# Hybrid encoder trunk on one core: even projections of two groups by seven products, two scan streams, division at the gates

## The chip, the core and the metric

The kernel runs on one core of a Trainium2 chip. The metric is device time of one execution in microseconds. All matrix work is float32 split into a rounded high part and a low part (`F32R`), so that one float32 product is three TensorE matmuls: high x high, high x low, low x high.

The engines are named as in the profile: PE is TensorE (PEld its weight loads), DVE is VectorE, ACT is ScalarE, POOL is GpSimd, SP is SyncE, whose queue issues every DMA.

## The reference

Two requests (2048 and 512 tokens, 1024 features) go through the same two layers. The first is the even one, the second the odd one:

```python
def even_sublayer(x, w_in, ...):
    u = x @ w_in
    qa, ka, va, za, gd, qb, kb, vb, zb = jnp.split(u, _offsets(EVEN_SPLITS), axis=-1)
    ya = gla_mixer(qa, ka, va, za, gd, ...)      # gated linear attention, chunks, both directions
    yb = swa_mixer(qb, kb, vb, zb, rel_bias, sink)   # softmax over |i-j| <= 128
    return jnp.concatenate([ya, yb], axis=-1) @ w_out

def swa_mixer(...):
    ...
    e = jnp.exp(s - m)
    p = e / (jnp.sum(e, -1, keepdims=True) + jnp.exp(sk - m))
    o = jnp.einsum('bnkgqs,bnskd->bnqkgd', p, vb)
    return o * jax.nn.silu(z)

def odd_sublayer(x, w_in, conv_w, w_out):
    bg, cg, h, z = jnp.split(x @ w_in, 4, axis=-1)
    conv = ...                                   # width-3 convolution of cg * h
    return (jax.nn.silu(z) * bg * conv) @ w_out

x = layer_norm(DN_ALPHA * x + sublayer(x))       # after each layer
```

## The kernel before

The 2560 tokens are five groups of 512 (0 to 3 the long request, 4 the short one) and 20 chunks of 128.

**Stages.** PE works through a list of dense stages (`run`, L2103). For each group of the even layer there are `tok` (`e1_tok`: values and decay inputs, 336-column matmuls) and `ch` (`e1_ch`: 21 channel units, each 24 matmuls of 512 columns against the group's transposed activations). `oe` and `oo` are the output projections of the even and the odd layer with residual and norm, `one` is the odd layer's input projection of group 4, and `pair` that of two groups at once. The order before is tok 4, ch 4, tok 3, ch 3, tok 2, ch 2, tok 1, ch 1, oe 4, tok 0, ch 0, one, oe 0, oo 4, oe 1, oe 2, pair 0, oe 3, oo 0, pair 1, oo 1, oo 2, oo 3.

**Pairs by seven products.** `odd_pair` computes a 2x2 block product (two halves of the inner dimension by two groups, two weight units) with seven half-size products instead of eight, in the order 1, 6, 7, 5, 2, 4, 3. Each product is 12 matmuls. `pair_weights` makes the sums of weight quarters and their high and low parts (ACT casts, POOL subtracts), `prep_pair` those of the activations.

**Side work.** Between dense matmuls the planner (`Flow`, L263) steps generators. `gla_stream` runs the scan: for each chunk, last to first, `inside` multiplies queries and keys by decays level by level (spans 1, 2, 4, 8, 16, 32, 64) on DVE, with small 32x32 and 64x64 matmuls for each level, then the chunk's output and state; `along` goes forward once all chunks of a request are through. `swa_front` computes scores and exponentials of a block (a chunk and one of two key heads; 40 in all) and divides by the row sum; `swa_back` transposes, multiplies by the values and then by the gates `gb` and stores to `mix_s`. `prep` loads transposed activations into three `pr` buffers and splits them into `st` tiles, of which there are eight: two groups' worth.

**What sets the order.** The planner has its own clocks for the engines; a generator is stepped when the data it named should be ready. The resulting order is fixed at build time on each engine. SP issues DMAs in that order, and one that waits holds all behind it. Stage gates are marks such as `gla_in3` (all inputs of group 3's scan stored), `swa_3` (chunk 3's attention stored), `bias` (the relative-bias tables loaded).

**Lines.** L242 is the helper through which every instruction of an engine is recorded, so all rows of the profile have this line; they are told apart by tile names: `acc` and `ps` are PSUM banks, `ws`/`y` raw weights, `wh`/`wl` their high and low parts, `md`/`pr` work buffers, `st` split activations, `QQ`/`KK` the scan's queries and keys, `P` attention probabilities, `den` their row sums.

## Time and profile before

| what | value |
|---|---|
| median of 3 runs | 2370.76 us (2369.61 to 2370.84) |
| profiled execution, its own time | 2370.12 us |
| span of that execution | 2368.1 us |
| PE busy | 2343.9 us (99%), 15830 records |
| DVE busy | 1582.8 us (67%) |
| ACT busy | 1226.1 us (52%) |
| POOL busy | 1418.4 us (60%) |
| granted TensorE clock | 0.998 of full speed |
| DMA | 437.37 MB, mean 185 GB/s |

The span runs from the first to the last instruction; the execution's own time has some 2 us around it. Busy shares are means over the whole run; a window table gives them by stage. A group's row has its count, its busy time and mean ns of one, then the idle time of the engine before these instructions and who ended it. A timeline row has start and length in us. DMA rows have the median time from issue to landing.

### The profile page before, as it was taken

Reading aid. Unit: us, or ns where it says so; the run is one execution under the profiler, and the core shown is the slowest. Engines: PE = TensorE matmul, PEld = TensorE weight load, DVE = VectorE, ACT = ScalarE, POOL = GpSimd, SP = SyncE. Lnnn points to the kernel's source line nnn. Section 1 sums busy time; section 2 is a strip of 40 time slices with the busy share of each in tenths; the row PEclk is TensorE's granted clock in tenths of the full one; section 3 lists DMA queues with packets and bytes.
Section 4 is the critical chain, followed back from the end, with each engine's and each line's share of the span. In section 5 each row is a group of like instructions: output and inputs, shape, how many; then the busy total and the mean of one; then the engine's idle time right before and its main releaser. Section 6 shows DMA issues by size and latency. Waiting matters only on the chain.

```text
span 2368.1 us, 43087 instructions
## 1 busy us (share of the span) xinstructions
PE 2343.9 (99%) x15830; PEld 1951.8 (82%) x15830; DVE 1582.8 (67%) x2699; ACT 1226.1 (52%) x2363; POOL 1418.4 (60%) x1610
## 2 busy tenths in 40 slices
PE   8999999999999999999999999999999999999998
PEld 8888889888988888888888888878888877888887
DVE  2267756767767677577776467876566587656567
ACT  4666776656576645665577532543334343333431
POOL 5454435443444444444444467898887689988674
PEclk9999999999999999999999999999999999999999
DMA  7977686676667657675478777232124633221573
GB/s 230 295 226 233 221 269 229 209 221 221 218 194 236 223 173 242 197 218 161 158 245 268 266 261 243 92 116 89 52 78 140 217 105 103 73 72 58 175 242 121
DMA packets 275057, 437.37 MB, mean 185 GB/s; under 512 B 21360, under 2 KB 160240, under 8 KB 274848
## 3 DMA queue, kind: packets, MB, share of 16 engines
q1 hardware_dynamic: 274848, 434.64, 56.5%
q8 instruction: 125, 2.05, 0.4%
q14 instruction: 84, 0.69, 0.1%
HBM read 319.72 MB, written 114.84 MB: 184 GB/s over the span
## 4 chain that ended last, share of the span: by engine, by line
PE 87%; DVE 5%; POOL 4%; DMA 2%; issue 1%; ACT 1%; SPq 0%; POOLq 0%; DVEq 0%; ACTq 0%
PE acc L242 71%; PE ps L242 17%; POOL wl L242 1%; POOL wh L242 1%; DVE st L242 1%; DVE bst L242 1%; DVE y L242 1%; POOL md L242 0%; SPq L242 0%; DVE QQ L242 0%; DVE P L242 0%; DVE KK L242 0%; DMA K<-kb_s 0%; DMA mix_s<-gb 0%; DMA op_s<-QQ 0%
## 5 line engine op out<-in xcount | busy, mean ns | idle before, releaser
L242 POOL TENSOR_TENSOR wl<-ws,wh 128x256 fp32r<-128x256 f32 (+1 forms) x912 | 750.7, 855 | 711.4 <-PE acc L242 478.0
L242 PE MATMUL acc<-st,wh 128*128 128x512 f32 x3160 | 828.5, 395 | 2.8 <-DVE pr L242 2.0
L242 PEld LDWEIGHTS acc<-st,wh 128*128 128x128 f32 x3160 | 580.9, 188 | 121.0 <-issue 3.1
L242 PE MATMUL acc<-st,wl 128*128 128x512 f32 x1744 | 471.9, 395 | 2.8 <-POOL wl L242 1.9
L242 PE MATMUL acc<-wh,st 128*128 128x512 f32 (+1 forms) x1680 | 389.4, 371 | 7.9 <-ACT st L242 6.4
L242 PEld LDWEIGHTS acc<-st,wl 128*128 128x128 f32 x1744 | 320.8, 188 | 68.0 <-POOL wl L242 4.1
L242 PEld LDWEIGHTS acc<-wh,st 128*128 128x128 f32 x1680 | 300.2, 189 | 55.1 <-ACT st L242 6.4
L242 ACT CAST wh<-ws 128x1024 fp32r<-128x1024 f32 (+2 forms) x252 | 249.0, 989 | 184.2 <-DMA ws<-in_w_oo 55.9
L242 PE MATMUL acc<-wl,st 128*128 128x512 f32 (+1 forms) x840 | 209.0, 368 | 0.6 <-POOL wl L242 0.5
L242 ACT ACTIVATE md<-md 128x512 f32<-128x512 f32 x264 | 164.7, 631 | 20.5 <-DVE md L242 14.9
L242 PEld LDWEIGHTS acc<-wl,st 128*128 128x128 f32 x840 | 150.7, 188 | 23.8 <-POOL wl L242 1.3
L242 DVE SCALAR_TENSOR_TENSOR md<-acc,md 128x512 f32<-128x512 f32 (+1 forms) x113 | 77.0, 683 | 81.5 <-ACT md L242 76.5
L242 DVE TENSOR_TENSOR st<-pr,st 128x512 fp32r<-128x512 f32 x115 | 98.5, 874 | 41.6 <-ACT st L242 41.2
L242 ACT ACTIVATE md<-acc 128x512 f32<-128x512 f32 (+1 forms) x133 | 76.2, 597 | 67.0 <-PE acc L242 66.5
L242 POOL TENSOR_TENSOR wh<-md,wh 128x256 fp32r<-128x256 f32 x118 | 96.7, 842 | 13.6 <-ACT wh L242 13.1
L242 ACT CAST pth<-ps 128x512 fp32r<-128x512 f32 x112 | 65.3, 583 | 73.1 <-PE ps L242 72.3
L242 DVE CUSTOM_DVE_ANT_0 P<-ps,P 128x384 f32<-128x384 f32 (+1 forms) x160 | 79.3, 525 | 29.6 <-PE ps L242 29.0
L242 ACT ACTIVATE P<-P,nm 128x385 f32<-128x385 f32 (+1 forms) x160 | 93.2, 587 | 3.9 <-DVE nm L242 3.9
L242 ACT ACTIVATE mv<-mv,eps 128x1 f32<-128x1 f32 x40 | 11.8, 295 | 151.8 <-DVE mv L242 147.7
L242 PE MATMUL acc<-P,wh 128*128 128x512 f32 x312 | 89.5, 400 | 0.4 <-POOL wh L242 0.4
L242 ACT COPY km<-KK 128x512 f32<-128x512 f32 x80 | 50.8, 635 | 72.2 <-DVE KK L242 50.9
L242 ACT CAST st<-pr 128x512 fp32r<-128x512 f32 x115 | 68.3, 617 | 30.3 <-DMA pr<-mix_s 12.9
(490 smaller groups left out, 4090.2 us busy)
## 6 DMA issues: line engine op xcount, KB each, us to landing
ws<-in_w_ch SPq DMA_DIRECT2D x105, 512.0 KB, 4.4
ws<-in_w_od SPq DMA_DIRECT2D x58, 512.0 KB, 4.2
ws<-in_w_oe SPq DMA_DIRECT2D x40, 512.0 KB, 3.8
ws<-in_w_oo SPq DMA_DIRECT2D x36, 512.0 KB, 3.5
K<-kb_s SPq DMA_DIRECT2D x32, 384.0 KB, 6.3
d_s<-md SPq DMA_DIRECT2D x40, 256.0 KB, 4.2
qb_s<-md SPq DMA_DIRECT2D x80, 128.0 KB, 3.9
tA<-d_s SPq DMA_DIRECT2D x20, 512.0 KB, 5.7
```

The source lines that it names most:

```text
L242: r = f(*a, **k)
```

## The change

**Seven products in the even layer.** Groups 4 and 3 now run together: tok 4, tok 3, then unit 0 of both groups plainly, then 20 units as ten pairs by seven products (`even_pair`), then tok 2 and the rest as before. `prep_even` loads the transposed activations of both groups once more, makes four sums per 128-row slab on DVE and their high and low parts. The parts are kept in the buffers of local attention (`P`, `Q`, `pth`, `ptl`, `gb`, `K0`, `K1`, `V`) until the last pair. `pair_weights` is made general for both uses and keeps fewer sums.

**The scan as two streams.** `inside` ends after the levels; a second generator `gla_behind` does the chunk's output and state. A chunk's levels can run while the chunk before is finished. Keys and queries may use `y` buffers, copies may use `md` buffers. Level 2's queries are copied aside, and the blocks of levels 2 and 4 are multiplied together into one PSUM bank, as those of 8 and 16 were already.

**Division at the gates.** The probabilities are no longer divided. The reciprocal row sums go to DRAM (`rd_s`), are read back as rows broadcast over 64 partitions, and POOL multiplies the gates by them.

Local attention's set-up also moves: its bias tables are loaded when products 6, 7 and 5 of the last pair are done. Other edits: the loop over late work is rewritten, a plain product holds its PSUM bank, `dtot` has eight columns.

The core of the diff:

```diff
+    def prep_even(self, a, b):
...
+        places = early + self.half
+        todo, raws, last = [(k, i, g) for k in range(4) for i in range(2) for g in (a, b)], [], []
...
+        for k in range(4):
...
+            b11, b12, b21, b22 = raws
+            t = self.take(places, (128, 512))
+            sub(t[:], b12[:], b11[:])
+            sub(b12[:], b22[:], b12[:])
+            sub(b22[:], b22[:], t[:])
+            sub(b21[:], b21[:], b22[:])
...
+            for n, r in ((6, b22), (7, b12), (5, t)):
+                hi[n].append(cell())
+                lo[n].append(cell())
+                split(n, k, r, None)
+                yield []
+        yield "plain_e"
+        hi[4], lo[4] = self.big_cells(), self.big_cells()
...
+    def even_pair(self, groups, units, take, put, decay):
...
+        for n, cts in enumerate(units):
+            u = {"ct": cts}
+            for i in (1, 6, 7, 5, 2, 4, 3):
+                if n == 0 and i in (4, 5, 6, 7):
+                    yield "paire_%d" % i
...
+                for k in range(4):
+                    c = slice(k * 128, k * 128 + 128)
+                    nc.tensor.matmul(p[:], w[:, 0, c], H[i][k], start=(k == 0), stop=False)
+                    nc.tensor.matmul(p[:], w[:, 0, c], L[i][k], start=False, stop=False)
+                    yield
+                for k in range(4):
+                    c = slice(k * 128, k * 128 + 128)
+                    nc.tensor.matmul(p[:], w[:, 1, c], H[i][k], start=False, stop=(k == 3))
...
     def setup_bias(self):
...
+        for i in (6, 7, 5):
+            yield "free_paire_%d" % i
...
     def inside(self, c, first, last, ld, K, ahead):
...
-            if s in (8,):
+            if s in (2, 8,):
...
+        self.heads.append((c, first, last, K, Q, base, acmp))
+        self.flow.mark("head_%d" % c)
...
     def swa_front(self):
...
-                for h in range(4):
-                    nc.vector.tensor_scalar(Pt[:, h, :w], Pt[:, h, :w], den[:, h:h + 1], None, op0=ALU.mult)
-                    if h == 1:
-                        yield []
+                nc.sync.dma_start(self.rd_s[c, kv].rearrange("h t -> t h"), den[:])
...
     def swa_back(self):
...
+            for j in range(4):
+                nc.sync.dma_start(rb[64 * kv:64 * kv + 64, 128 * j:128 * j + 128],
+                                  self.rd_s[c, kv, j:j + 1].broadcast_to([64, 128]))
...
+            yield [gb, rb]
+            flat = gb[:].rearrange("p h t -> p (h t)")
+            nc.gpsimd.tensor_tensor(flat, flat, rb[:], op=ALU.mult)
...
     def run(self):
...
-        stages = [("tok", 4), ("ch", ((4,), A + B)), ("tok", 3), ("ch", ((3,), A + B)),
+        even = [(1, 2), (3, 4), (5, 6), (7, 8), (13, 14), (15, 16), (9, 10), (11, 12), (17, 18), (19, 20)]
+        stages = [("tok", 4), ("tok", 3), ("ch", ((4, 3), [0], even)),
                   ("tok", 2), ("ch", ((2,), A + B)), ("tok", 1), ("ch", ((1,), A + B)), ("oe", 4),
```

**How the order moves, first place: PE and SP at the first channel units.** PE before, from the end of the first token projection (`gd` are the decay inputs, `y` the decay weights):

```order
L242 MATMUL acc<-wl,st 128x336 x2
L242 MATMUL acc<-st,wh 128x512 x16
L242 MATMUL acc<-st,wl 128x512 x8
L242 MATMUL acc<-ident,gd 32x128 x4
L242 MATMUL acc<-st,wh 128x512 x16
```

PE in the changed kernel, from the end of group 3's token projection; `relb` is the relative bias, and `P`, `Q`, `gb` hold the sums of slabs 0 and 1, 2, and 3:

```order
L242 MATMUL acc<-wl,st 128x336 x2
L242 MATMUL acc<-st,wh 128x512 x16
L242 MATMUL acc<-st,wl 128x512 x8
...
L242 MATMUL acc<-st,wh 128x512 x8
L242 MATMUL ps<-QQ,relb 8x512
L242 MATMUL acc<-st,wh 128x512 x4
L242 MATMUL acc<-P,wh 128x512 x4
L242 MATMUL acc<-Q,wh 128x512 x2
L242 MATMUL acc<-gb,wh 128x512 x2
```

The plain units are followed at once by products of sums, and the relb matmul stands inside product 1. SP in the changed kernel at that place (`S`, `A` and `pr` receive the last slab; `KK` is the bias line):

```order
L242 DMA relb<-in_relb 32x8
L242 DMA pr<-in_xT 128x512
L242 DMA S<-in_xT 128x512
L242 DMA A<-in_xT 128x512
L242 DMA k_s<-md 128x4x128
L242 DMA line_s<-KK 8x512
L242 DMA pr<-in_xT 128x512
```

In the order before, the line's store stands among the stores of the first token projection and no activations are loaded here. The fourth load of the last slab now stands behind it.

**Second place: SP at oe 0.** Before, where the last result of `one` (`od_s`) is stored (`tA`, `QQ` and the like are the forward scan's loads):

```order
L242 DMA ws<-in_w_oe 128x1024
L242 DMA pr<-od_s 128x512 x3
L242 DMA P<-in_x 128x1024
L242 DMA od_s<-md 128x512
L242 DMA mix_s<-KK 512x1x128
```

In the changed kernel:

```order
L242 DMA pr<-mix_s 128x512 x3
L242 DMA ws<-in_w_oe 128x1024
L242 DMA mix_s<-qn 512x1x128
...
L242 DMA rd_s<-den 128x4x1
L242 DMA od_s<-md 128x512
L242 DMA QQ<-op_s 128x512
L242 DMA QQ<-qf_s 128x512
L242 DMA qn<-ga_s 128x512
L242 DMA pr<-mix_s 128x512
L242 DMA pr<-od_s 128x512
```

Before, all eight loads of `mix_s` for oe 0 stand ahead of this piece and the `pr` buffers already serve the next stage; now three stand just ahead of it and five behind the last `od_s` store, among loads of `od_s`.

More of the change, by code (lines that the diff above doesn't have):

```diff
@@ L296, in flush @@
     def flush(self, everything=False, name=None):
-        now, keep = [], []
-        for one in self.late:
-            (now if everything or name in one[2] or (name is None and one[0] <= self.t) else keep).append(one)
-        self.late = self.model.late = keep
+        now = [one for one in self.late if everything or name in one[2] or (name is None and one[0] <= self.t)]
         for one in now:
-            one[1]()
+            if any(one is x for x in self.late):
+                self.late[:] = [x for x in self.late if x is not one]
+                one[1]()
     def force(self, *tiles):
@@ L804, in prep @@
         raws = []
-        eager, homes = homes is not None, homes or self.half
+        eager, homes = homes is not None, homes or self.half + (self.mids if wide else [])
         todo = list(range(8))
@@ L1034, in e1_tok @@
         gd = self.gd[g] = self.sm((128, 4, 32), "gd")
-        stores = {"gla_in": 24, "swa_in": 29, "done_sw": 33, "done_e1_": 37}
+        names = ["gla_in", "swa_in", "done_sw", "done_e1_"] if g < 3 else ["gla_in", "done_e1_", "swa_in", "done_sw"]
+        stores = {n: 24 + sum({"swa_in": 5}.get(x, 4) for x in names[1:i + 1]) for i, n in enumerate(names)}
         def left(what):
@@ L1075, in e1_ch @@
         if us[0] == 0:
-            if groups == (4,):
+            if 4 in groups:
                 yield "up"
@@ L1150, in take @@
                           lambda: put(g, dst, h, o, "done_e1_" if u < 17 else "done_sw"))
-            if 1 < u < 10:
-                decay(g, (u - 2) // 4, (u - 2) % 4)
+            for i in () if units else {7: (6, 7)}.get(u, (u - 1,) if 0 < u < 7 else ()):
+                decay(g, i // 4, i % 4)
         for u in us:
@@ L1161, in e1_ch @@
                 yield
-            if u == 9:
+            if u == 7 and not units:
                 self.drop(up, *(G[g] for g in groups))
@@ L1165, in e1_ch @@
                 G.clear()
+        if units:
+            own = self.owned["e1_%d" % groups[1]]
+            self.drop(*own[:2])
+            del own[:2]
+            flow.mark("plain_e")
+            yield from self.even_pair(groups, units, take, put, decay)
         if u == 16:
@@ L1178, in gla_load, with gla_home @@
         return q, T1
+    def gla_home(self, tag):
+        done = self.flow.done
+        rows = "late_e1_1" in done and "res_x1_4_3" not in done
+        return [(self.e2, tag, 1)] if rows or self.model.spare(tag, 1) else self.large[:1]
     def gla_load_k(self, c):
-        K = self.e((128, 2, 512), "KK")
+        K = self.take(self.gla_home("KK"), (128, 2, 512))
         for i in range(2):
@@ L1232, in inside @@
         base = None
-        Sb = self.bst if not last else None
         wait = []
@@ L1314, in inside, with load_v, behind @@
                     nc.vector.copy_predicated(acmp[:], self.lmask[:, lt].unsqueeze(1).broadcast_to([128, 4, 32]), x)
-            if s == 4:
-                v = self.e((128, 512), "v")
-                nc.sync.dma_start(v[:], self.v_s[c])
+            if s in (4, 32):
+                ahead(s)
             yield [Q] if s < 16 else [Q, K]
-        end = tots[128]
+        nc.vector.tensor_copy(self.dtot[:, c], mk(tots[128], 0, [[1, 8]]))
+        self.heads.append((c, first, last, K, Q, base, acmp))
+        self.flow.mark("head_%d" % c)
+    def load_v(self, c):
+        v = self.e((128, 512), "v")
+        self.nc.sync.dma_start(v[:], self.v_s[c])
+        return v
+    def behind(self, c, first, last, K, Q, base, acmp, v, ahead):
+        nc = self.nc
+        Sb = self.bst if not last else None
         A = self.e((128, 4, 128), "A")
@@ L1349, in inside @@
                                   acmp[:].unsqueeze(2).broadcast_to(wide))
+        self.open -= 1
         if not first:
-            yield from self.bank()
+            yield from place()
             kb = turn(1)
-        ahead(1)
+        self.drop(K)
         yield [A, v] + ([Sb] if Sb is not None else [])
@@ L1452, in seq, with gla_behind, ahead @@
         return (0, 16) if g < 4 else (16, 20)
+    def gla_behind(self):
+        nxt = []
+        for c in [*range(19, 15, -1), *range(15, -1, -1)]:
+            yield "head_%d" % c
+            v = nxt.pop() if nxt else self.load_v(c)
+            def ahead():
+                if c not in (0, 16) and "gla_in%d" % ((c - 1) // 4) in self.flow.done:
+                    nxt.append(self.load_v(c - 1))
+            yield from self.behind(*self.heads.pop(0), v, ahead)
+            v = None
     def gla_stream(self):
+        nxt = {}
@@ L1900, in total @@
             def total(name, x, y, op):
-                while self.free_at(self.mids) > flow.t:
-                    yield 0.3
-                t = sums[name] = self.take(self.mids, (128, 512))
                 c = self.model.clock
                 e = nc.gpsimd if c["gpsimd"] + 0.6 < c["vector"] else nc.vector
+                if name in (3, 7):
+                    e.tensor_tensor(y, x, y, op=op)
+                    sums[name] = y
+                    yield [m[1] if name == 7 else held[0]]
+                    return
+                places = self.mids if p != "e" or n == 0 else self.half + (self.early if n < 4 else self.large)
+                while self.free_at(places) > flow.t:
+                    yield 0.3
+                t = self.take(places, (128, 512))
+                held.append(t)
+                sums[name] = t[:]
                 e.tensor_tensor(t[:], x, y, op=op)
@@ L1912, in pair_weights @@
                     yield from total(5, quarter(1, 0), quarter(1, 1), ALU.add)
-                    yield from total(6, sums[5][:], quarter(0, 0), ALU.subtract)
+                    yield from total(6, sums[5], quarter(0, 0), ALU.subtract)
                 elif i == 7:
```

298 lines of the change are left out of this document (240 added, 58 removed).

## Prediction

> **What bounds the kernel now.** I read the profile in this order: the page's busy times, the table by stages, the chain of waits, the groups by form, the waits of each engine, then the timeline at two stage entries. The span and the busy times come first.
>
> ```profile
> span 2368.1 us, 43087 instructions
> PE 2343.9 (99%) x15830; PEld 1951.8 (82%) x15830; DVE 1582.8 (67%) x2699; ACT 1226.1 (52%) x2363; POOL 1418.4 (60%) x1610
> ```
>
> TensorE (PE) is busy for 2343.9 of 2368.1 us. The 24.2 us left are not a reserve in the middle: the first matmul starts at 6.44 us and the last ends at 2360.3, which leaves some 10 us for all waits between.
>
> ```profile
> 6.44 0.65 PE L242 MATMUL acc<-wh,st 128*128 128x336 f32 x1 [6.44 <-ACT st L242]
> 2359.90 0.40 PE L242 MATMUL acc<-P,st 128*128 128x512 f32 x1
> ```
>
> The table by stages (window; then busy us of PE, PEld, DVE, ACT, POOL; clock; DMA share; GB/s) says the same of every stage. The four windows are the first channel projections, the next 200 us, the main part of the attention, and the first stage of the odd layer that already uses seven products.
>
> ```profile
> 60.00:160.00 100.00, 100.00 (x672) 81.58 (x671) 41.37 (x71) 63.27 (x99) 52.43 (x69) 1.00 0.88 275
> 160.00:360.00 200.00, 200.00 (x1746) 171.58 (x1745) 135.13 (x314) 139.42 (x314) 86.74 (x112) 1.00 0.73 232
> 760.00:1300.00 540.00, 538.89 (x4352) 450.83 (x4351) 387.46 (x790) 328.59 (x724) 240.47 (x294) 1.00 0.65 209
> 1551.00:1886.00 335.00, 334.73 (x1460) 274.76 (x1461) 210.30 (x255) 129.41 (x187) 278.12 (x288) 0.99 0.32 108
> ```
>
> PE fills each of them; DVE never has over 72% of a window (387 of 540), and POOL is near its limit only in the last (278 of 335). So a microsecond of matmul that goes is a microsecond won, as long as no new wait stands in its place, and relief of DVE alone is worth nearly nothing. What one 512-column matmul costs is read from the chain of waits (start, length, what), in that last window:
>
> ```profile
> 1551.27 334.56 PE acc L242 x1456
> ```
>
> 334.56 / 1456 = 0.230 us each. (The 395 ns of the groups overlap, since matmuls are pipelined.)
>
> **What the change removes.** Twenty of the 21 channel units of groups 4 and 3 were 2 x 20 x 24 = 960 matmuls of 512 columns; ten pairs of units at seven products of 12 matmuls are 840. The other TensorE work (token projections, scan blocks, scores, transposes) keeps its counts and shapes. 120 x 0.230 = 27.6 us go. The profiled execution took 2370.12 us (its span and 2.0 around it; the median of the runs is 2370.76, 0.6 above), so the bare sum is 2342.5 us. Everything else has to be hidden or added. Edits that move no time go together: the new loop over late work, held PSUM banks in the plain products, eight columns of decay totals, decays one unit earlier, the order of the marks.
>
> **The first 85 us: 0.** Group 3's activations now have to be there when group 4's token projections end, and 16 more slabs of 256 KB are loaded for the sums.
>
> ```profile
> 0.00:60.00 60.00, 53.40 (x284) 48.10 (x285) 16.54 (x33) 25.56 (x42) 34.18 (x56) 1.00 0.72 229
> ```
>
> By the changed SP queue, loads and stores up to the entry add up to about 22 MB in 85 us, 260 GB/s. The rows of before show 229 in the first 60 us and 275 in the next 100 with PE full; so it fits, and what it costs if it doesn't is the landing time in the next part.
>
> **Entry of the seven products: +7.5 us.** The product order is 1, 6, 7, 5, 2, 4, 3. Product 1 uses plain activations; product 6 needs the sums of all four column slabs of xT. In the changed SP queue the last slab's last load stands behind the store of the relative-bias line, and that store waits for a DVE add, which waits for the small relb matmul; PE has that matmul in the middle of product 1. The rows that price this chain:
>
> ```profile
> 37.72 0.68 DVE L242 TENSOR_TENSOR pth<-ps,gb 8x512 f32<-8x512 f32 x1 [0.87 <-PE ps L242]
> 40.24 0.39 SPq L242 DMA_DIRECT2D line_s<-pth  x1
> pr<-in_xT SPq DMA_DIRECT2D x35, 256.0 KB, 4.7
> md<-in_xT SPq DMA_DIRECT2D x5, 256.0 KB, 6.5
> L242 DVE TENSOR_TENSOR st<-pr,st 128x512 fp32r<-128x512 f32 x115 | 98.5, 874 | 41.6 <-ACT st L242 41.2
> ```
>
> From the end of the relb matmul: 0.68 (the add, 37.72), 0.39 (the store's issue, 40.24), 4.7 from the load's issue to its landing, then in DVE's order two subtractions that make the sum, one that is queued between, and the low half, 4 x 0.87 = 3.5. That is 9.3, with some 0.5 for five hand-offs 9.8. PE still has four matmuls of product 1 and six of product 6 to do, 2.3 us; 7.5 us of wait remain. No row shows this wait, as the stage isn't there. A wait of PE can't be below 0; at most the landing takes 6.5, as in the slowest group of xT loads, and DVE comes 3 us late: 12. I take the sum of the medians.
>
> **Entry of the first output projection after the odd layer's group 4: +6 us.** Local attention now starts when the products release the P buffers, near 300 us instead of at 126 (its bias tables were loaded there), and still has 40 blocks to do; before, its last store was at 1261. The projection's loads of mix_s now stand behind the 18th of attention's 20 stores. Before (timelines of SP and PE):
>
> ```profile
> 126.15 0.98 SPq L242 DMA_DIRECT2D P<-bias_s  x2
> 1261.09 0.53 SPq L242 DMA_DIRECT2D mix_s<-gb  x1
> 1263.46 1.60 SPq L242 DMA_DIRECT2D pr<-mix_s  x3
> 1287.44 1.37 SPq L242 DMA_DIRECT2D pr<-mix_s  x1
> 1310.95 0.33 SPq L242 DMA_DIRECT2D ws<-in_w_oe  x1
> 1321.02 0.32 SPq L242 DMA_DIRECT2D od_s<-md  x1
> 1319.65 3.90 PE L242 MATMUL acc<-wh,st 128*128 128x512 f32 x16
> 1326.12 3.79 PE L242 MATMUL acc<-wh,st 128*128 128x512 f32 x16
> pr<-mix_s SPq DMA_DIRECT2D x40, 256.0 KB, 4.8
> L242 ACT CAST st<-pr 128x512 fp32r<-128x512 f32 x115 | 68.3, 617 | 30.3 <-DMA pr<-mix_s 12.9 <-DMA pr<-od_s 7.0 <-DMA pr<-in_xT 6.5
> ```
>
> The eight loads went out from 1263 to 1288, 32 to 56 us ahead of the stage at 1319.65. Now three stand just ahead of the stage's second weight load (at 1310.95, 8.7 us ahead): landing, cast and low half take 4.8 + 0.62 + 0.87, 6.3 in all, so these come in time. The fourth stands behind the last od_s store (1321.02, 1.4 after the start) and three more loads of about 0.4: issued at 2.7, ready at 9.0. The stage wants it when its second weight block begins, 6.5 after the start (1326.12). That is 2.5 us. The other four stand further back, between weight loads, and share three pr buffers with the next stage's od_s loads; I give the two later pairs 1.7 each. Sum some 6. From below, 0, if the loads find their buffers early; from above, if each of three pairs is a whole landing late, 14.
>
> **Weights in the new stage: 0, hidden.** POOL now makes 140 low halves and 22 sums there. Rows for the halves and the sums:
>
> ```profile
> L242 POOL TENSOR_TENSOR wl<-ws,wl 128x256 fp32r<-128x256 f32 x44 | 48.1, 1113 | 12.3 <-ACT wl L242 12.0
> L242 POOL TENSOR_TENSOR wh<-y,wh 128x256 fp32r<-128x256 f32 x32 | 37.5, 1194 | 2.0 <-ACT wh L242 1.8
> L242 POOL TENSOR_TENSOR wl<-QQ,wl 128x256 fp32r<-128x256 f32 x10 | 13.6, 1377 | 4.3 <-ACT wl L242 4.3
> L242 POOL TENSOR_TENSOR wh<-md,wh 128x256 fp32r<-128x256 f32 x118 | 96.7, 842 | 13.6 <-ACT wh L242 13.1
> L242 POOL TENSOR_TENSOR md<-ws,md 128x512 f32<-128x512 f32 x9 | 11.7, 1297 | 0.0
> ```
>
> By the names in the changed order half of them read from y at about 1.2 us, the rest at 0.84 to 1.11: 140 x 1.09 + 22 x 1.30 = 181 us, against 840 x 0.230 = 193 of products and some 10 of side matmuls. 22 us of PE hide what POOL lacks in evenness. If each half took the longest row, 1.38, POOL would need 222 and the stage would be 19 us longer; that is a rival. The Trainium skill, in "SBUF — State Buffer", section "Who interferes with whom", says that a DVE instruction with two SBUF inputs and a GpSimd instruction that reads SBUF exclude each other for their whole length. The trace agrees in kind (the same 128x256 form takes 842 ns in one group and 1377 in another), and by that rule the scans, which now run beside this stage, would bring that rival's time.
>
> **Local attention: 0.** Per block four DVE divisions go:
>
> ```profile
> L242 DVE TENSOR_SCALAR P<-P,den 128x384 f32<-128x384 f32 x128 | 61.6, 543 | 1.1
> L242 DVE TENSOR_SCALAR P<-P,den 128x256 f32<-128x256 f32 x32 | 10.9, 405 | 0.3
> L242 POOL TENSOR_TENSOR gb<-gb 128x512 f32<-128x512 f32 x20 | 27.3, 1367 | 61.4 <-DVE gb L242 61.4
> ```
>
> 72.5 us of DVE go, and 20 POOL multiplications of 1.37, 27 us, come. Both lie beside PE; the relief can win at most the 10 us of waits that PE has, and if POOL's cover in the attention were gone (240 of 540 us busy), the 27 would show. I take neither. SP gets 40 stores of reciprocals and 160 short loads. At about 0.4 us each that is 80 us of issue in 1000, and a read waits on SP until its store has landed; weight loads queue behind. What they have in reserve:
>
> ```profile
> SPq L242 <- POOL wl L242: 490.1, 195, 7.4
> SPq L242 <- DVE den L242: 9.1, 3, 4.5
> ACT wh L242 <- DMA ws<-in_w_ch: 43.0, 19, 7.2
> ```
>
> SP mostly waits for a weight buffer to come free (490 us), so loads go out as early as they can; and ACT has waited 43 us for such weights without PE feeling it. From below nothing is won; from above half a microsecond per block, 20 us. I take 0, as the nearest row (SP waiting 9.1 us in all for den) is small. The Trainium skill, in "DMA: Bandwidth & Descriptors", section "Rules for kernel authors", says that a strided last dimension is lowered to one descriptor per element; the reciprocals are stored that way, 512 elements of four bytes. No run here shows such a store.
>
> **The scans: 0.** They start in the middle of the new stage instead of at about 110 us, as two streams; levels 2 and 4 make one PSUM bank instead of two. Their matmul count stays and no long stretch of the new order has scan work without projection matmuls between. Their cover is DVE's 28% in the attention; if that were gone, the wait would show at the entry priced above.
>
> Sum: 2370.1 - 27.6 + 7.5 + 6 = 2356.0 us.
>
> **The rivals.** One: no new wait. Loads land sooner and DVE runs ahead; PE stays as full as in the windows above. 2370.1 - 27.6 = 2342.5, say 2343. For it: in the trace of before entries cost next to nothing. Against it: the order of the SP queue, which no speed of DVE changes. Two: POOL sets the pace of the new stage. If the halves take 1.25 on average, POOL needs 140 x 1.25 + 29 = 204, no cover is left and unevenness shows: 10 to 19 us, so 2366 to 2375, about the time of before. For it: the y and QQ rows; against it: 278 of 335 us in the like stage, where PE lost nothing. Three, on the other side: SP held by reciprocals. Where a read stands close behind its own store, SP waits up to a landing, 4 us, and weight loads come late. From 0.5 us of PE per block on (2375.5 - 2356 = 19.5 over 40) the kernel is slower than before; at 0.75 it takes 2386. For it: the changed order puts reads as near as three rows behind their store; against it: SP's reserve above.
>
> **How the numbers follow.** A measurement of this kernel can tell about 0.2%, 4.7 us: faster is below 2366.0, slower above 2375.5. Chances: forecast 0.58, no new wait 0.15, POOL 0.15, SP 0.12. Faster: the first two and a fifth of the third, 0.76. Same: the rest of the third, 0.12. Slower: 0.12. The range from 2342 to 2372 takes in the first two cases with their bounds and most of the third; outside lie the SP case and the top of POOL's, under 0.2.
>
> **What would show it.** Right: the page's PE records of 512 columns down by 120 (each counts once), PE's busy time near 2316; one idle time of PE of 5 to 10 us between 80 and 100 us, released by DVE (the low half in gb); idle times at the start of the projection near 1300, released by DVE st. Wrong: no such gaps (rival one), PE waiting for POOL wl or wh between 100 and 300 us (two), ACT wh waiting for weights and PE behind it through the local attention, 300 to 1300 us (three). A total above 2375 makes the forecast wrong whatever the gaps.

## The result and the profile after

The changed kernel takes 2554.0 us (median of 4 runs, 2550.9 to 2558.2), the kernel before 2370.2 beside it: a ratio of 1.0777 (95% interval 1.0761 to 1.0793). The forecast was 2356, from 2342 to 2372: wrong in sign and by 198 us. The page's first lines of the changed kernel:

```profile
span 2556.4 us, 43218 instructions
PE 2377.4 (93%) x15710; PEld 1968.1 (77%) x15710; DVE 1621.4 (63%) x2659; ACT 1244.6 (49%) x2431; POOL 1472.3 (58%) x1628
...
DMA packets 307972, 435.39 MB, mean 170 GB/s; under 512 B 44928, under 2 KB 193792, under 8 KB 307760
```

The 120 matmuls are gone (15830 to 15710), yet PE is busy for longer: 2377.4 us in place of the expected 2316.3, and idle for 179.0 in place of 24.2. So the 188.3 us between the two spans are -27.6 (matmuls), +154.8 (PE idle) and +61.1 (the same matmuls busy for longer). Most of the 61.1 is a lower clock: in windows of 2 us, PE's busy time times what the granted clock lacks of full speed adds up to 52.4 us, and to 1.6 before. What the other 10 us are is not shown. The table by stages, with the windows of the prediction, says where:

```profile
60.00:160.00 100.00, 93.35 (x414) 75.85 (x413) 58.38 (x84) 63.67 (x115) 58.56 (x69) 0.97 0.69 214
160.00:360.00 200.00, 183.71 (x1775) 151.15 (x1774) 167.51 (x259) 118.08 (x213) 126.76 (x130) 0.98 0.57 173
760.00:1300.00 540.00, 484.03 (x4558) 402.23 (x4559) 345.39 (x719) 293.93 (x608) 206.60 (x250) 0.95 0.78 187
1551.00:1886.00 335.00, 331.48 (x1480) 271.74 (x1479) 238.91 (x292) 128.64 (x211) 277.33 (x279) 1.00 0.44 147
```

The loss is in the attention (third row): PE has 484 of 540 us, its clock 0.95 in place of 1.00, and no other engine is full. The DMA engines are busier than before (0.78 for 0.65) and move less (187 GB/s for 209). PE's waits between 300 and 1300 us have no one releaser, only many small ones (the first five rows):

```profile
PE acc L242 <- ACT wh L242: 16.3, 5, 8.3
PE ps L242 <- DVE acmp L242: 11.1, 1, 11.1
PE ps L242 <- issue: 11.1, 8, 2.7
PE acc L242 <- ACT md L242: 9.8, 2, 7.2
PE ps L242 <- DMA pr<-x_s: 9.7, 4, 5.4
```

The new wait of SP, from the waits of its queue:

```profile
SPq L242 <- DMA rd_s<-den: 113.4, 24, 9.9
```

SP stands behind these stores 24 times, for up to 9.9 us. In twelve of the 24 the loads of the reciprocals are next in its queue and go out 8.8 to 13.1 us after the store's issue (a store of 2 KB; the slowest group used in the prediction landed in 6.5). In the other twelve it is the eighth DMA behind the store, whatever that is, which goes out only when the store has landed; why the eighth is not shown. The first wait in the timeline of SP, and four rows of the table in steps of 2 us behind that store:

```profile
356.11 0.37 SPq L242 DMA_DIRECT2D rd_s<-den  x1
356.53 0.50 SPq L242 DMA_DIRECT2D V<-vb_s  x1
357.08 0.46 SPq L242 DMA_DIRECT2D gb<-gb_s  x1
367.43 2.40 SPq L242 DMA_DIRECT2D md<-rd_s  x4
```

```profile
360.00:362.00 2.00, 2.00 (x18) 2.00 (x17) 0.11 (x1) 0.05 (x1) 0.16 (x1) 1.00 0.09 17
...
366.00:368.00 2.00, 2.00 (x15) 2.00 (x15) 0.18 (x1) 0.14 (x2) 1.51 (x3) 1.00 0.19 27
...
372.00:374.00 2.00, 0.00 (x0) 0.00 (x0) 0.00 (x0) 0.03 (x1) 0.00 (x0) 1.00 0.76 246
...
376.00:378.00 2.00, 1.04 (x2) 0.54 (x2) 0.00 (x0) 0.00 (x0) 0.00 (x0) 0.50 0.88 288
```

SP stands still from 357.5 to 367.4, hardly any data move, PE runs dry at 370 and waits 5.0 us, and when the work comes back PE's clock is 0.50 for some 5 us. (The Trainium skill, in "TensorE: Matmul & The Clock Gate", Part 1, says that PE runs at half its clock after an idle window of about 3.4 us; the row of 0.50, behind that wait of 5.0 us, agrees.)

Averaged over all 40 stores, worked out from such windows of 1 us, the data rate (GB/s) by the time from the store's issue:

```
us from issue    -3   -2   -1    0    1    2    3    4    5    6    7    8    9   10   11   12   13
change          245  230  209  203  202  185  148   93   76   44   41   42   47   77  128  207  248
```

On average a store takes the transfers of the whole core down to a fifth for some five microseconds. Two theories of that were put against each other, SP that waits (it issues nothing in the meantime) and DMA engines that choke on the store itself (512 elements of four bytes), and a third, that the scans and the local attention, which start 200 us later, are too crowded.

### The profile page after: what moved, and what is told of

It reads as the page before. It is cut to its first block, busy times and chain, and to the rows that moved or that the text cites. A ratio compares the mean times of both kernels' runs of the same rounds, so it can differ in the third digit from the quotient of the medians.

```text
span 2556.4 us, 43218 instructions
## 1 busy us (share of the span) xinstructions
PE 2377.4 (93%) x15710; PEld 1968.1 (77%) x15710; DVE 1621.4 (63%) x2659; ACT 1244.6 (49%) x2431; POOL 1472.3 (58%) x1628
## 5 line engine op out<-in xcount | busy, mean ns | idle before, releaser
L242 POOL TENSOR_TENSOR wl<-ws,wh 128x256 fp32r<-128x256 f32 (+1 forms) x752 | 613.1, 846 | 801.8 <-ACT wh L242 320.2
L242 PE MATMUL acc<-st,wh 128*128 128x512 f32 x2760 | 740.5, 402 | 26.8 <-ACT wh L242 15.0
L242 PEld LDWEIGHTS acc<-st,wh 128*128 128x128 f32 x2760 | 519.1, 192 | 135.0 <-ACT wh L242 16.3
L242 PE MATMUL acc<-st,wl 128*128 128x512 f32 x1592 | 431.5, 399 | 3.5 <-issue 1.2
L242 PE MATMUL acc<-wh,st 128*128 128x512 f32 (+1 forms) x1696 | 398.8, 374 | 24.2 <-ACT st L242 16.8
L242 ACT CAST wh<-ws 128x1024 fp32r<-128x1024 f32 (+2 forms) x227 | 216.2, 952 | 322.4 <-DMA ws<-in_w_ch 116.5
L242 ACT ACTIVATE md<-md 128x512 f32<-128x512 f32 (+1 forms) x287 | 179.3, 631 | 32.8 <-DVE md L242 26.0
L242 PE MATMUL acc<-P,wh 128*128 128x512 f32 x420 | 120.2, 398 | 0.4 <-POOL wh L242 0.4
L242 POOL TENSOR_TENSOR wh<-y,wh 128x256 fp32r<-128x256 f32 x96 | 97.5, 1035 | 26.6 <-ACT wh L242 26.6
L242 PEld LDWEIGHTS acc<-P,wh 128*128 128x128 f32 x420 | 78.7, 189 | 20.0 <-POOL wh L242 2.1
L242 POOL TENSOR_TENSOR wh<-ws,wh 128x256 fp32r<-128x256 f32 x78 | 72.9, 955 | 35.9 <-ACT wh L242 35.6
```

The source lines that it names most:

```text
L242: r = f(*a, **k)
```

## Experiments

**First four: which part of the change.** The edits, in order; the first takes the division back to the weights as before (the loads and the gates' multiplication go with it):

```
-  nc.sync.dma_start(self.rd_s[c, kv].rearrange("h t -> t h"), den[:])
+  for h in range(4):
+      nc.vector.tensor_scalar(Pt[:, h, :w], Pt[:, h, :w], den[:, h:h + 1], None, op0=ALU.mult)
```

> The changed kernel with the softmax division back on the weights (four DVE multiplications per block, no reciprocals in DRAM, no GpSimd multiplication of the gates); seven products, the two scan streams and the new start of local attention stay. Theory A (the stores of the reciprocals, 512 elements of four bytes each, choke all 16 DMA engines: around the 40 stores the data rate falls from a mean of 245 GB/s to 42 for some five microseconds): 2345 to 2365 us, PE's idle time between 300 and 1600 us from 150 us down to under 25. Theory B (the loads of the reciprocals hold the SP queue until their store has landed, 113 us in 24 waits): the same, 2345 to 2365. Theory C (scans and local attention start some 200 us later and are crowded into the rest of the attention): 2480 us or more, since nothing of the crowding goes.

Measured: 2387.5 us (1.0078, 1.0063 to 1.0093). 166 of the 184 us hang on the division at the gates, so the crowding is not the main thing: PE's idle time between 300 and 1600 us is 26.0 us, in place of 141.4 in the change. But the kernel is still 19 us slower than before, where A and B had it faster. More on that below.

```
+  nc.tensor.transpose(pr[:4, :128], den[:], self.ident[:])
+  nc.scalar.copy(dr[:], pr[:4, :128])
-  nc.sync.dma_start(self.rd_s[c, kv].rearrange("h t -> t h"), den[:])
+  nc.sync.dma_start(self.rd_s[c, kv], dr[:])
```

> The changed kernel, but the reciprocals are first turned by one small transposition on PE and one copy on ACT, so that the store writes four rows of 512 bytes; the loads, their wait for the store and the multiplication of the gates stay. Theory A: 2350 to 2385 us, and no dip of the data rate behind the stores. Theory B: a store of rows still has to land, about 4 us instead of 10, so that some 45 of the 113 us of waiting stay and the time is 2420 to 2470 us. Theory C: 2540 to 2560 us.

Measured: 2420.8 us (1.0218, 1.0203 to 1.0233). No dip of the data rate is left (between 185 and 258 GB/s around the stores) and SP waits 9.9 us in all for rows to land. 133 us at least are the form of the store. The time misses A's range by 36 us, and lands in B's, though not for B's reason: the waits for the store were 9.9 us, not 45. The 40 transpositions bring costs of their own (0.27 us each on PE; PE sits 8.6 us ahead of them until a reciprocal is there; SP waits 72.9 us for the copies).

```
-  self.rd_s[c, kv, j:j + 1].broadcast_to([64, 128])
+  self.I['xT'][0, 0, j:j + 1, 0, 0:128].broadcast_to([64, 128])
```

> The changed kernel, but the broadcast loads read rows of the input xT in place of the reciprocals (the gates are scaled by wrong numbers): as many loads of the same size, none of which waits for a store; the 40 element stores stay. Theory A: 2500 to 2550 us, with the same dips of the data rate behind the stores. Theory B: 2350 to 2390 us. Theory C: 2530 to 2560 us.

Measured: 2523.0 us (1.0654, 1.0636 to 1.0671): 31 us less than the change, in the range of A. No load waits for its reciprocals here, yet SP's waits for the stores are only halved (113.4 us in the change):

```profile
SPq L242 <- DMA rd_s<-den: 58.8, 22, 6.4
```

In all 22 it is the eighth DMA behind the store that waits. Behind the other 18 stores, which hold nothing, the mean data rate falls to 39 GB/s all the same, so the dip does not come from SP waiting for the store. Behind the store at 434.31 SP goes on issuing loads, and the table shows what the DMA engines make of them:

```profile
436.00:438.00 2.00, 2.00 (x11) 1.62 (x10) 2.00 (x6) 2.00 (x4) 1.01 (x2) 1.00 1.34 312
438.00:440.00 2.00, 2.00 (x11) 1.65 (x10) 0.79 (x2) 1.94 (x6) 1.88 (x3) 1.00 1.35 39
440.00:442.00 2.00, 2.00 (x10) 1.68 (x9) 0.38 (x1) 1.90 (x10) 0.00 (x0) 1.00 1.16 40
...
448.00:450.00 2.00, 0.08 (x1) 0.00 (x0) 0.00 (x0) 1.24 (x2) 0.07 (x1) 1.00 1.04 397
```

The share, which adds up the time of all packets, is 1.16 to 1.35, and for four microseconds the engines move 40 GB/s: busy with something slow. Ten microseconds later PE has nothing to do. Not every store looks so full: averaged over the 40, the share between 5 and 10 us behind the store is 0.70 at 50 GB/s, and behind the change's first store it was 0.09 to 0.24, though that store took eleven microseconds to land. What is slow on the way from the engines to DRAM is not shown.

In the kernel before, the store in place of the division, and the loads and the gates' multiplication as in the change:

```
-  nc.vector.tensor_scalar(Pt[:, h, :w], Pt[:, h, :w], den[:, h:h + 1], None, op0=ALU.mult)
+  nc.sync.dma_start(self.rd_s[c, kv].rearrange("h t -> t h"), den[:])
```

> The kernel before with only the division moved to the gates, word for word as in the change (element stores, broadcast loads, GpSimd multiplication); no seven products in the even layer, scans and local attention as before. Theories A and B: 2500 to 2570 us, PE idle by some 120 us or more between 126 and 1270 us. Theory C: 2365 to 2385 us.

Measured: 2573.1 us (1.0860, 1.0842 to 1.0878). This is 3 us above the range of A and B. The division at the gates alone makes the old kernel 204 us slower, with the same dips (37 GB/s six microseconds behind the store). Theory C falls.

**What makes the store slow.** First the number of pieces: 16 bytes for each partition (128 pieces) in place of four times four (512).

```
-  self.rd_s[c, kv].rearrange("h t -> t h")
+  self.rd_s[c, kv].rearrange("h (a b) -> (h a) b", b=4)
```

> The changed kernel with each store of reciprocals written as 128 pieces of 16 bytes in place of 512 of four (the order in DRAM is another, so the gates are scaled by the wrong reciprocals); loads, waits and all else as in the change. The kernel with rows of 512 bytes took 2420.8, the change 2554.0. Theory A1 (the price is one per written element): a quarter of the 133 us between them stays, 2445 to 2470 us. Theory A2 (any write under 512 bytes costs a store the same whatever its number of pieces, since the memory has to be read and merged): 2540 to 2560 us. Theory A3 (only the number of bytes per partition matters and 16 bytes are as small as four): the same as A2.

Measured: 2388.0 us (1.0067, 1.0050 to 1.0084). All three variants of A missed: not a quarter of the price stays, but nothing, and small pieces as such are not dear. The SP queue of this run waits for the store as follows, and the page's first lines are:

```profile
SPq L242 <- DMA rd_s<-den: 15.8, 8, 4.3
```

```profile
span 2386.1 us, 43218 instructions
PE 2328.3 (98%) x15710; PEld 1936.8 (81%) x15710; DVE 1628.1 (68%) x2659; ACT 1246.5 (52%) x2431; POOL 1485.0 (62%) x1628
```

Against the change PE is idle 121.2 us less and busy 49.1 less at a better clock: the whole difference. Then 512 pieces of four bytes again, at other distances; all four runs read xT in the broadcast loads, like the run with 2523.0.

```
   "rd_s" shape                       store
   (NC, 2, 128, 4, 2)                 self.rd_s[c, kv, :, :, 0]                              # 8 bytes apart
   (NC, 2, 4, 128, 16)                self.rd_s[c, kv, :, :, 0].rearrange("h t -> t h")      # 64 apart
   (NC, 2, 4, 128, 4), (.., 8)        the same                                               # 16, 32 apart
```

> The changed kernel with broadcast loads that read the input xT (as in the run where no load waits for a store, 2523.0 us) and with the element store written to another place: 512 pieces of four bytes, but the four of one partition lie 8 bytes apart, 32 bytes for each partition. With 16 contiguous bytes for each partition the whole price was gone (2388.0). Theory P1 (the price is that of 512 pieces, or of pieces of four bytes, wherever they lie): 2500 to 2545 us with the dip of the data rate behind the stores. Theory P2 (neighbours in DRAM come from different partitions and so from different DMA engines, and writes into the same short line of DRAM have to go one after the other): 2375 to 2400 us and no dip, since a partition's pieces now lie together.

> The same, with the pieces in the order of the change (each head's 128 values in a row over the partitions), but 64 bytes from one piece to the next, so that no two pieces share a line of 64 bytes. Theory P1: 2500 to 2545 us. Theory P2: 2375 to 2400 us. Theory P3 (it is the walk itself, four far places for each partition): as slow as P1 here, while the run with 8 bytes between pieces is fast.

> As the run with 64 bytes from piece to piece, but 16: four pieces, from four partitions, share 64 bytes, and two share 32. Theory L64 (the price comes from pieces that share 64 bytes, and goes by how many): between 2400 and 2460 us. Theory L32 (they must share 32 bytes): 2390 to 2415 us, as two share here what in the run with 8 bytes between the pieces of a partition nobody shared. Theory M (it is a threshold, such as 4 bytes in a row): 2385 to 2391 us.

> 32 bytes from piece to piece: two pieces, from two partitions, share 64 bytes, none shares 32. Theory L64: 2393 to 2415 us, about what two partitions to 64 bytes cost before (2408.1). Theory L32 and theory M: 2385 to 2391 us, as with 64 bytes.

Measured, by the distance from piece to piece, with the ratio's interval and the lowest mean data rate behind the stores:

```
distance  neighbours from       us        ratio (95% interval)       lowest GB/s
 4 bytes  other partitions    2523.0    1.0654 (1.0636 to 1.0671)       39
 8 bytes  same partition      2408.1    1.0165 (1.0146 to 1.0184)      118
16 bytes  other partitions    2389.2    1.0087 (1.0072 to 1.0102)      189
32 bytes  other partitions    2388.6    1.0083 (1.0066 to 1.0100)      205
64 bytes  other partitions    2387.6    1.0074 (1.0057 to 1.0091)      208
```

P1 falls: 512 pieces of four bytes are free from 16 bytes apart on. P3 falls with the run of 64 bytes, and P2 at 8 bytes, where it had no dip. The runs with 64 bytes and with 4 differ in nothing but these addresses, and 135.4 us lie between them. Their packets are the same to the last one; first the run with 64 bytes, then that with 4:

```profile
DMA packets 307972, 435.39 MB, mean 183 GB/s; under 512 B 44928, under 2 KB 193792, under 8 KB 307760
...
q1 hardware_dynamic: 307760, 432.64, 55.8%
```

```profile
DMA packets 307972, 435.39 MB, mean 173 GB/s; under 512 B 44928, under 2 KB 193792, under 8 KB 307760
...
q1 hardware_dynamic: 307760, 432.64, 60.4%
```

55.8% of 2385.7 us against 60.4% of 2519.5: 191 us more of all 16 engines, some 3050 us of engine time over 20480 pieces, 0.15 us for each, if all of it is put down to the pieces (other packets slowed beside them would be in it). With 64 bytes the share between 5 and 10 us behind the store is 0.71, as with 4, but at 230 GB/s in place of 50. L64 falls (four pieces to 64 bytes, or two, cost nothing). L32 misses at 16 bytes by 0.8 us only, less than the runs of one kernel differ by; there is no dip there either. M is left, with a threshold between 4 and 16 bytes and a residue at 8. Whether what counts is two pieces in one 16 bytes, or eight and more in one 64, these runs don't tell: both orders agree with them. P2's reason, different partitions, isn't shown either: at 8 bytes the pieces that lie in one 16 bytes come from the same partition and still cost 20 us.

**The loads of the reciprocals.** Rows again, with the loads moved to the end of a block; then 16 bytes for each partition with one load of 2 KB for each of 64 partitions, which the gates' multiplication reads with a step:

```
-  for j in range(4):
-      nc.sync.dma_start(rb[64 * kv:64 * kv + 64, 128 * j:128 * j + 128], self.rd_s[c, kv, j:j + 1].broadcast_to([64, 128]))
+  nc.sync.dma_start(rb[64 * kv:64 * kv + 64], self.rd_s[c, kv:kv + 1].broadcast_to([64, 512]))
...
+  nc.gpsimd.tensor_tensor(gb[:], gb[:], rb[:].rearrange("p (t h) -> p h t", h=4), op=ALU.mult)
```

> The kernel that stores the reciprocals as rows (2420.8 us), with the four loads of a block issued at the end of the block in place of its beginning. Theory B (what is left of the gate path, 33 us over the kernel with the division on the weights, is SP waiting for the rows to land): SP's waits for rd_s under 10 us and 2390 to 2403 us. Theory H (it is the loads themselves, 160 issues of some 0.7 us on SP and 40 transpositions and copies): 2412 to 2425 us.

> The changed kernel with the reciprocals stored as 16 bytes for each partition and read back by one load for each block in place of four (64 times the 2 KB of the block), the multiplication of the gates reading them with a step; the output is the right one. Theory B (SP's time is on the path): 120 issues of some 0.7 us less on SP give 2374 to 2383 us. Theory I (SP is not on the path once the stores don't choke the DMA): as the run with 16-byte stores and the one with the division on the weights, 2384 to 2391 us.

Measured: 2410.1 us (1.0162, 1.0146 to 1.0177), 11 less than with early loads, a third of the 33; it lies below H's range and above B's, so neither holds alone. And 2430.3 (1.0255, 1.0240 to 1.0270), which neither theory had: 120 issues fewer and 42 us more than with 16-byte stores and four loads (2388.0). Its table by stages:

```profile
1200.00:1300.00 100.00, 94.13 (x712) 78.48 (x707) 66.92 (x148) 59.38 (x154) 35.84 (x40) 0.93 0.65 213
1300.00:1400.00 100.00, 82.05 (x400) 65.68 (x401) 62.16 (x141) 66.39 (x214) 31.28 (x34) 0.91 0.75 247
1400.00:1500.00 100.00, 89.77 (x417) 74.18 (x416) 70.49 (x97) 42.60 (x109) 54.83 (x58) 0.95 0.78 269
```

The loss is at the end of the attention. The multiplication that reads with a step is not it: 1.62 us in place of 1.43, twenty times. The planner, which has fewer SP issues to place, made another order: one block of local attention stores its reciprocals between 800 and 900 us (three with four loads), eleven between 1200 and 1400 (eight). What in its rules does that was not followed.

**The remaining 18 us.** The kernel with 16-byte stores stands 18.0 us above the span of before: -27.6 of matmuls, +33.6 of PE idle time (57.8 for 24.2) and +12.0 of matmuls that are busy for longer (8.5 of these by the granted clock, in windows of 2 us). By windows of 100 us the idle time is 6.4 more in the first, 8.8 between 100 and 300, 7.4 between 300 and 400, 5.7 from 400 to 1200 and 5.1 from 1300 to 1400. Three sites, and a run for each, all with the division on the weights: the store of the relative-bias line later, the scans later, and the odd layer's projection ahead of the even layer's, so that scans and attention have longer.

```
   setup_bias:   -  yield "up"; yield 2.0     +  yield "paire_5"
   gla_stream:      yield "early"             +  yield "free_paire_6"
   stages:       -  ("oe", 0), ("oo", 4)      +  ("oo", 4), ("oe", 0)
```

> The kernel with the division back on the weights (2387.5 us), in which the relative-bias line is made only after the sums for products 6, 7 and 5 are there, so that the last xT load no longer stands behind the store of that line. Theory D (the order of the SP queue makes PE wait 5.5 us at the entry of the seven products, at 93 us, and some 3 more by the lower clock behind the gap): that gap under 1.5 us and 2378 to 2384 us. Theory E (the gap is DVE's, which has too much to do there): the gap stays over 4 us and the time is 2385 to 2391.

Measured: 2386.5 us (1.0063, 1.0049 to 1.0078), in E's range and 1.0 us from the run without this edit, less than the runs differ by. The old wait is gone, another, shorter one stands in its place: the matmul of the relative bias now waits for its own late load.

```profile
PE ps L242 <- DMA relb<-in_relb: 3.0, 1, 3.0
```

With the loads early and only the matmul late, on top of the one-load kernel:

> The kernel of the run before, in which the matmul of the relative bias and the store of its line are held back until the sums for products 6, 7 and 5 are there, while its three loads stay where they were. Theory D (the wait of 5.5 us at the entry of the seven products, released by the last xT load behind the line's store, is worth its length and some 3 us of lower clock): no PE wait over 2 us between 80 and 110 us, and 6 to 9 us less than the run before. Theory E (it is given back by later waits): within 3 us of the run before.

Measured: 2426.5 us (1.0244, 1.0228 to 1.0259), 3.7 less than without, the intervals overlap; the wait is 4.4 us in place of 6.0, so D's condition was not met. The waits of SP between 80 and 92 us show why:

```profile
SPq L242 <- DVE Q L242: 2.4, 1, 2.4
```

The last xT load has no store of the line ahead of it any more and still waits 2.4 us, for DVE to be done with the slab 2 half in `Q`. So D's reason, the line's store, is not what holds it. What the entry is worth when its wait is gone altogether stays open.

> The kernel with the division back on the weights (2387.5 us), in which the scan streams wait until the last pair's product 6 is done, so that no scan runs beside the seven products. Theory F (DVE, 91 of 100 us busy between 200 and 300, is the bound there, and PE loses 10 us to scans whose QQ and A come late): PE idle between 100 and 300 us under 3 us. If nothing is given back: 2373 to 2380 us. Theory G (the scans are only moved into a tighter attention): the same gaps come back later, above all before the first output projection near 1320, and the time is 2385 to 2420 us.

Measured: 2392.6 us (1.0088, 1.0074 to 1.0102). DVE's load beside the products falls from 91 to 62 of 100 us and PE loses 1.2 us there in place of 8.8, as F said; and it comes back, as G said: 5.6 and 12.6 us of idle time at the end of the attention, where the kernel without this edit has 0.5 and 9.2:

```profile
200.00:300.00 100.00, 98.85 (x514) 82.31 (x513) 62.08 (x86) 59.87 (x102) 68.35 (x78) 1.00 0.60 182
...
1200.00:1300.00 100.00, 94.41 (x502) 80.13 (x501) 67.47 (x158) 64.55 (x193) 34.09 (x43) 0.95 0.69 238
1300.00:1400.00 100.00, 87.39 (x427) 70.53 (x426) 64.73 (x138) 63.31 (x200) 35.12 (x43) 0.93 0.76 249
```

In the next four the exchange of the two projections also changes something of what is computed for them (which part was not traced); the number of matmuls is the same.

> The kernel with the division back on the weights (2387.5 us), in which the odd layer's output projection of group 4 comes ahead of the even layer's output projection of group 0, so that scans and local attention have some 23 us more before their results are read. Theory J (they end too late, since they start 200 us later, and PE pays 9 us of waits and 5 of lower clock between 1310 and 1350 us): PE idle between 1300 and 1400 us under 4 us, and 2373 to 2380 us. Theory K (the wait only passes to the projection that now stands there, since its input has just been stored): 2384 to 2395 us.

> The run before with the matmul of the relative bias and its line's store held back until the sums for products 6, 7 and 5 are there. If the entry's wait was given back at the first output projection, it is now won: 4 to 9 us less than the run before. If it is given back elsewhere: within 3 us of it.

> The run with the odd layer's projection first, and the scan streams held until the last pair's product 6 is done. Held back alone, the scans took PE's idle time between 100 and 300 us from 11 to 1 us and lost it again between 1200 and 1400 us (22 us there in place of 10). Theory J: with more time before the results are read, at most half of that is lost again, 2364 to 2375 us. Theory K: 2384 to 2400 us, with the same waits between 1200 and 1400 us.

> All three together: the odd layer's projection first, the scans held back, the relative bias held back. Theory J: the three sites add up, 2356 to 2368 us, faster than the kernel before. Theory K: 2380 us or more.

Measured: 2404.2 us (1.0147, 1.0131 to 1.0163), 2400.7, 2402.2 and 2398.6 (1.0121, 1.0104 to 1.0138). J falls; K is missed by 9 us in the first and by 2 in the third; holding the relative bias back is worth 3.5 us there, between its two theories. The attention doesn't end earlier against its deadline; the planner lets it run on, its last softmax sum at 1406 us in place of 1351, and the waits pass to the window after. Of the run with the exchange alone:

```profile
1400.00:1500.00 100.00, 86.04 (x351) 68.64 (x350) 56.50 (x74) 31.02 (x53) 45.26 (x53) 0.90 0.62 218
```

No kernel that was run beats the one before.

## Why the prediction was wrong

**Local attention, "0": this step failed.** It said: "From below nothing is won; from above half a microsecond per block, 20 us. I take 0, as the nearest row (SP waiting 9.1 us in all for den) is small." Measured: 166 us with the division at the gates against the division on the weights, 4.2 us per block; 135 of them go when the same pieces lie 64 bytes apart. The nearest row was the wrong one: it is a wait for a tiny engine result, not for a transfer, and none of the rows shown has a transfer of four-byte pieces. (That wait grew to 67.5 us in the run with 16-byte stores, which still took 2388.0.) The bound from above was taken from what SP would lose, with a landing of 4 us, and not from what such a store does to all other transfers. The prediction had the fact in hand (512 elements of four bytes, and the Trainium skill's rule in "DMA: Bandwidth & Descriptors", section "Rules for kernel authors", of one descriptor per element, which the packets now bear out: 23568 more under 512 bytes than before, 20480 of them these), noted that no run shows such a store, and gave it no price. A cost that no row shows deserves a wide bound, and it got a narrow one. Without this step the forecast would still have missed: 2387.5 us lies 15.5 above its range, by the scans and the clock below.

**The third rival (0.12)** had the sign and a part: SP held by its own reads, 0.75 us per block. Its sign showed as well: between 300 and 1300 us ACT waits 110.9 us for channel weights, 43.0 in the whole kernel before. Taking the reads' wait away alone gave 31 us, 0.78 per block. The other 135 come with the addresses of the pieces; how much of them is slow transfers and how much SP standing at the eighth DMA (58.8 us) was not separated. Its chance was too low and its price had only the smaller part of the mechanism.

**Matmuls, -27.6: right.** The profile has 120 fewer, 15710. In time it can be checked to a few us: PE's busy time times the granted clock, in windows of 2 us, is 2342.3 us before, 2318.2 with 16-byte stores and 2316.4 with the division on the weights, 24 to 26 less.

**Entry of the seven products, +7.5: place and size right, the chain only in part.** In the changed kernel's timelines of SP, DVE and PE, and in the waits of SP between 84 and 88 us:

```profile
84.38 0.29 SPq L242 DMA_DIRECT2D line_s<-KK  x1
...
86.68 0.33 SPq L242 DMA_DIRECT2D pr<-in_xT  x1
...
85.09 1.56 DVE L242 TENSOR_TENSOR Q<-pr,Q 128x512 fp32r<-128x512 f32 x1
...
90.94 0.69 DVE L242 TENSOR_TENSOR S<-pr,S 128x512 f32<-128x512 f32 x1 [1.42 <-DMA pr<-in_xT]
...
93.06 1.52 PE L242 MATMUL acc<-gb,wh 128*128 128x512 f32 x2 [5.86 <-ACT gb L242]
...
SPq L242 <- DVE Q L242: 1.9, 1, 1.9
```

The load stands 2.3 us behind the line's store and lands in 4.3; PE waits 5.9 us, at the place named, for the high half in gb rather than the low one. But the store is not what holds the load last: SP waits 1.9 us more for DVE, whose low half in `Q` reads a `pr` buffer until 86.65, and the load into `pr` goes out at 86.68. The prediction had no term for that buffer. That the wait's length is also won back when it goes is not shown: of the two runs that tried, one brought in a new wait and one took only a quarter of it away.

**Entry of oe 0, +6: right in kind, with the late attention around it.** PE waited 9.0 us there in the change (1.5, 5.8 and 1.8 us between 1482 and 1524, released by ACT st) and 4.1 with the division on the weights (ACT st and DVE st); with the scans' and the attention's own late results the 100 us from 1300 on have 9.2 us of idle time there.

**Scans, "0": wrong by some 9 us.** Beside the seven products, with their sums and differences, DVE is busy 91 of 100 us (75 before), and PE waits for the scans' QQ. The row before, then the row and the wait with the division on the weights:

```profile
200.00:300.00 100.00, 100.00 (x956) 82.58 (x955) 75.30 (x165) 69.79 (x135) 45.83 (x53) 1.00 0.70 217
...
200.00:300.00 100.00, 92.58 (x975) 73.51 (x974) 91.20 (x134) 52.23 (x92) 68.54 (x64) 1.00 0.52 154
...
PE ps L242 <- DVE QQ L242: 6.1, 8, 1.7
```

The argument ("their cover is DVE's 28% in the attention") used the room of another stage than the one into which they were moved. And the later start, which the prediction noted, has a price of its own at the end of the attention, which the edits tried here moved and did not remove.

**Weights, 0: right.** POOL is busy 67 and 68 of 100 us in the new stage, and PE never waits for it there, so rival two did not come, nor what was drawn from the rule beside it: the low halves took 0.74 to 1.01 us, by the means of their groups between 100 and 300 us, where that rule's rival had 1.38 and rival two 1.25. Whether the 842 and 1377 ns of before differ by that rule is not shown.

**The clock: a term that was missing.** Gaps of PE are followed by a stretch at a lower clock: by the windows of 2 us, 51 us for 155 of idle time in the change, 8.5 for 34 with 16-byte stores. A predicted wait should be charged with a quarter to a third more.

## What to carry to other kernels

Cost a DMA by its pieces and their addresses, not by its bytes or its issue time: a store of 2 KB that scatters four-byte elements into neighbouring places slowed all transfers of the core to a fifth for several microseconds, and the same elements 16 bytes apart, or 16 contiguous bytes for each partition, cost nothing that could be measured. Where a kernel runs at 99% of one engine, 40 small stores are enough to lose six times what 120 matmuls bring (166 us against 27.6). Work that starts later must still end by the same place: look for the cover in the stage it moves into and at its deadline, not on average.

## What the runs showed of the hardware

- Pieces of four bytes, four bytes apart and from different partitions: 0.15 us of a DMA engine more for each than 64 bytes apart, and the data rate of the whole core falls to 40 GB/s on average. From 16 bytes apart on there is no dip.
- The Trainium skill, in "DMA: Bandwidth & Descriptors", section "Specifications", gives 512 bytes as the least transfer for full rate, with reads and merges below. Here pieces of 4 and 16 bytes, so placed, left the time at 2388 to 2389; what mattered was what lies beside a piece.
- The DMA share alone does not show such a store: behind it the share is 0.70 at 50 GB/s, with pieces 64 bytes apart 0.71 at 230 GB/s.
- SP's eighth DMA behind such a store waits until the store has landed, in all 22 waits of the run with 2523.0 us and in 12 of the 24 of the change.
